# The convolution half of an encoder's output product on two scaled fp16 parts per operand, with its weight rows loaded raw

## The chip, the cores and the metric

The kernel runs on one core of a Trainium2 chip. A core has a matrix engine (TensorE, PE in the profile), a vector engine (VectorE, DVE), a scalar engine (ScalarE, ACT), a general engine (GpSimd, POOL) and a sync engine (SyncE, SP) that here only issues transfers. Each engine runs its own instructions in order; semaphores hold an instruction back until what it reads is there and what it overwrites is no longer needed. Transfers run on 16 DMA engines; in this kernel SP issues the plain ones and POOL those that change the type or add into their target, each in a queue of its own.

The metric is device time in microseconds of one execution. The time before is the median of three.

## The reference

The reference is an encoder trunk of two layers in float32 (1024 positions, width 1024). What matters here is the second half of the mixer: eight attention heads make 512 channels, a convolution module makes the other 512, and their concatenation is multiplied by w_o:

```python
u = a * jax.nn.sigmoid(gt)
u = _dwconv(u, w_dw_conv[l], b_dw_conv[l])
u = jax.nn.silu(_layernorm(u, g_conv_ln[l], b_conv_ln[l]))
y = jnp.concatenate([y_attn, u], axis=-1) @ w_o[l].astype(h.dtype)
x = x + y
h2 = _rmsnorm(x, g_ffn[l])
z = _dwconv(h2 @ w_up[l].astype(h2.dtype), w_dw_ffn[l], b_dw_ffn[l])
```

The stage that changes is `u` times the lower 512 rows of w_o, and its sum with x.

## The kernel before, in words

Activations lie with channels on the 128 partitions and the 1024 positions along the free axis, in two column halves of 512. A product in full precision is made of three products: each operand is split into a high part and the remainder (low part), and high×high, high×low and low×high are summed in PSUM. Parts are either f32r (a float32 form that PE takes, shown as `fp32r` where an engine writes it and `f32` at PE) or fp16 pairs with a power-of-two scale.

A layer has four stages. **Project** (`project`; in the profiled execution about 0 to 200 us in layer 0, 1095 to 1295 in layer 1) makes the queries, keys and the gated convolution input, section by section (q0, q1, q2, then k0, k1 ...). While it runs, VectorE applies the taps of the depthwise convolution (`conv_step`), and some taps are made on ScalarE and added into the tile by a POOL transfer (`tap_far`, tile `far`). A clock of planned PE time (`clock["pe"]`) decides when weights are asked for: `supply` issues a cast (POOL transfer, `cast`) LEAD ahead of need and turns it into a pair TURN ahead (`complete`). **Attention** (to 410 and 1505 us) makes the heads' outputs `ys`. The **output stage** (`feed`, from `wo_steps`; 410 to 496 us and 1505 to 1590 us) is a list of steps: `steps[n]()` emits PE's work of step n, and then everything that was `put` at (n, rank) is emitted in order of rank. Order of emission is each engine's order. The **up and down products** follow in the same list.

The steps of the output stage are: heads of the first column half in steps 0 to 3 (step 0 is done earlier, in attention), heads of the second half in 4 to 6, convolution blocks of the first half in 7 to 10, the last heads block in 11, convolution blocks of the second half in 12 to 15. Each block makes two of the eight 128-row output tiles: per tile 4 channel blocks times 3 parts, 12 matmuls of 512 columns (`accumulate`, L979 to L985), tile `po`. After a heads block VectorE adds x to it (`add_heads`, L1019); after a convolution block it adds it into the same tile (`evict`, L1023), which is stored, squared on ScalarE and summed for the next norm.

The weights of both halves come as f32r pairs made by POOL and ACT. `cast_pair` (L944) takes a 128×2×512 tile, and a POOL transfer writes the cast to its first half; `complete` (L201 to L204) has ScalarE write the negative of it to the second half (L202), and a second POOL transfer adds the source into that (L203). The heads' half (part 1, tag `m`, 8 slots) is cast in attention, from step WO_AT of its own agenda on, and the last ones are completed at step −1 of the list. The convolution half (part 0, tag `ws`, 8 slots) is cast at steps 0 and 1, rank 5, and completed at steps 2 and 3, rank 2. In the same steps SP loads rows of w_up (`fetch`, L1134, tile `wu`), whose squares give scales (`first_squares`).

The convolution operand comes from `conv_norm` (from L2013): `mean` and `square` at step 0, sums at 1 and 2, the root of the variance (`rstd`, tiles `lnr0t`, `lnr0v`) at step 3, its spread over the partitions (`lnr0s`) at step 4, then per column half `scale` (L2044, VectorE, then SiLU on ScalarE), `close` (L2048, ScalarE, high part `us_jh`) and `rest` (L2053 to L2055, VectorE, low part `us_jl`). Each `us` part is a float32 tile of 1024 columns under tag `b`.

Tags are slots of SBUF that are used in turn: `b` has 31 of them for most 1024-column tiles, `ws` 8, `m` 8, `wr` 3 (SLOTS, L59). The step products `scales` (L911 to L928) find the scale of the value weights and of the next norm's gain from sums of squares that `weight_squares` (L894) and the matmul with ones made; all of it at section n2 of project.

What a planner decides is only the clock in project; in the output stage the order is written by hand in steps and ranks.

Of the kernel before, what the change touches and what calls it, by code (L numbers as in the profile page):

```python
# [9 lines left out]
F32 = mybir.dt.float32  # L10
# [7 lines left out]
T = 1024  # L18
# [54 lines left out]
END_TURNS = 1  # L73
P_SCALE = 32768.0
# [64 lines left out]
class Encoder:  # L139
# [274 lines left out]
    def first_sections(self, l, supply):  # L414
# [14 lines left out]
        nc.scalar.activation(out=self.cp.tile([128, 1], F32, name="table"), in_=self.ones[:, 0:1], func=AF.Square)  # L429
# [83 lines left out]
        nc.gpsimd.tensor_copy(out=self.cp.tile([128, 1], F32, name="held"), in_=x[2][:, 0:1])  # L513
# [46 lines left out]
    def project(self, l, carry):  # L560
# [10 lines left out]
        qk = self.cp.tile([128, 8], F32, name=f"qk{l}", tag="qk", bufs=1)  # L571
        col = lambda i, n=1: qk[:, i:i + n]
# [42 lines left out]
        def launch(steps, n=-1):  # L615
            active.append([clock["pe"], steps, n])
# [229 lines left out]
        scales = {1: lambda: st.update(squares=self.weight_squares(l, w["v"])),  # L846
                  2: lambda: st.update(scale=self.scales(l, st.pop("squares")))}
# [21 lines left out]
        gain_squares()  # L869
        launch(gate(0), -3)  # L870
# [21 lines left out]
        return u, conv, away, (qd, qrd, kd, krd), (kvs, w["v"], st["scale"]), heads  # L892

    def weight_squares(self, l, w):  # L894
        nc, par = self.nc, self.par[l]
        f = self.cp.tile([128, 20], F32, name=f"sc{l}", tag="sc", bufs=1)
# [4 lines left out]
        nc.scalar.activation(out=f[:, 8:16], in_=par[:, P_GFFN:P_GFFN + 8], func=AF.Square, accum_out=f[:, 2:3])  # L901
        return f
# [8 lines left out]
    def scales(self, l, f):  # L911
        nc = self.nc
        ps = self.bank(f"sc{l}p", (128, 3))
        nc.tensor.matmul(ps, self.ones, f[:, 0:3], start=True, stop=True)
        col = lambda i: f[:, i:i + 1]
        nc.vector.tensor_copy(out=f[:, 2:5], in_=ps)
        nc.vector.tensor_tensor(out=col(3), in0=col(2), in1=col(3), op=ALU.add)
        self.half_exponent(f[:, 5:7], f[:, 3:5])
        self.power(col(0), col(5), -1.0, 200.0)
        self.power(col(1), col(5), 1.0, 39.0)  # L920
        self.power(col(7), col(6), -1.0, 197.0)
        nc.vector.tensor_scalar(out=col(16).bitcast(I32), in0=col(6).bitcast(I32), scalar1=EXPONENT, scalar2=-20.0 * EXPONENT,
                                op0=ALU.mult, op1=ALU.add)
        nc.vector.tensor_copy(out=col(17), in_=col(16).bitcast(I32))
        nc.vector.tensor_scalar(out=f[:, 8:16], in0=self.par[l][:, P_GFFN:P_GFFN + 8], scalar1=col(7), scalar2=None, op0=ALU.mult)
        nc.vector.tensor_scalar(out=col(18), in0=col(17), scalar1=-2.0 ** 31, scalar2=None, op0=ALU.add)
        self.gs, self.back, self.nback = f[:, 8:16], col(17), col(18)
        return col(0), col(1)  # L928

    def layer(self, l, carry):  # L930
        with self.psum(f"mix{l}", ([f"w{i}" for i in range(3)], 1), 2):
            mixed = self.project(l, carry)
        with self.psum(f"attn{l}", 2, 4):
            casts, ready = {}, {}
            ahead = {WO_AT: lambda: [casts.update({m: self.wo_cast(l, m, 1)}) for m in range(4)],
                     **{58 + m: lambda m=m: ready.update({(1, m): self.complete(*casts.pop(m))}) for m in range(3)},
                     61: lambda: (ready.update({(1, 3): self.complete(*casts.pop(3))}), [casts.update({m: self.wo_cast(l, m, 1)}) for m in range(4, 8)])}
            begun = {"x": {}, "po": {}}
            begun["turn"] = lambda: ready.update({(1, m): self.complete(*casts.pop(m)) for m in range(4, 4 + END_TURNS)})
            conv, ys = mixed[1], self.attention(l, *mixed, ahead, ready, begun)  # L940
        with self.psum(f"ffn{l}", 0, ([f"d{i}" for i in range(8)], 1)):
            return self.feed(l, conv, ys, ready, casts, begun["x"])()
# [10 lines left out]
    def feed(self, l, conv, ys, ready, casts, x):  # L953
# [6 lines left out]

        self.wo_steps(l, conv, ys, ready, casts, x, steps, put)
# [25 lines left out]
    def wo_steps(self, l, conv, ys, w, casts, x, steps, put):  # L987
# [33 lines left out]
        def evict(c, m):  # L1021
            xm = x[m, c]
            nc.vector.tensor_tensor(out=xm, in0=ps.pop((c, m)), in1=xm, op=ALU.add)  # L1023
# [699 lines left out]
    def attention(self, l, u, conv, away, spill, kvs, loaded, ahead, wo, begun):  # L1723
# [7 lines left out]
        def rows(tt):  # L1731
            (kv, wv, _), ts = kvs, slice(tt * 128, (tt + 1) * 128)
# [280 lines left out]
    def conv_norm(self, l, conv, out, put):  # L2013
# [34 lines left out]
        def close(j, c):  # L2048
            if c == 0:
                out.append([self.blk(f"us{l}_{j}{i}", F32R) for i in "hl"])  # L2050
            nc.scalar.copy(out=out[j][0][:, HALVES[c]], in_=st[j, "z"][:, HALVES[c]])

        def rest(j, c):  # L2053
            hi, lo = (t[:, HALVES[c]] for t in out[j])
            nc.vector.tensor_tensor(out=lo, in0=st[j, "z"][:, HALVES[c]], in1=hi.bitcast(F32), op=ALU.subtract)  # L2055
# [84 lines left out]
```

## Time and profile before

| | us |
|---|---|
| median of three runs | 2208.74 |
| lowest and highest of them | 2208.42, 2209.5 |
| the profiled execution | 2208.39 |
| its span | 2206.6 |
| mean granted clock of PE | 0.999 |

The profile is one execution. Its page gives busy times by engine, the span in 40 slices, the DMA queues, the chain of work that ended last and the costliest groups of instructions; further views give a timeline of each engine, the instructions of a line or tile, and busy time by stretch. In a group the form is `line engine operation out<-in, partitions x elements and type, count | busy us, mean ns of one | idle time before them, what ended it`. A matmul's duration overlaps its neighbours', so its rate is read from start to start. `[3.67 <-PE lnr0t L278]` behind a timeline row says that the engine stood idle for 3.67 us and that PE's work of line 278 on tile lnr0t ended this. The page's row of the w_o transfers:

```profile
wo<-in_w_o POOLq DMA_DIRECT2D x64, 256.0 KB, 7.4
```

These are 16 per half and layer: eight casts and eight adding transfers, 7.4 us from issue to landing in the median.

### The profile page before, as it was taken

Reading aid. Unit: us, or ns where it says so; the run is one execution under the profiler, and the core shown is the slowest. Engines: PE = TensorE matmul, PEld = TensorE weight load, DVE = VectorE, ACT = ScalarE, POOL = GpSimd, SP = SyncE. Lnnn points to the kernel's source line nnn. Section 1 sums busy time; section 2 is a strip of 40 time slices with the busy share of each in tenths; the row PEclk is TensorE's granted clock in tenths of the full one; section 3 lists DMA queues with packets and bytes.
Section 4 is the critical chain, followed back from the end, with each engine's and each line's share of the span. In section 5 each row is a group of like instructions: output and inputs, shape, how many; then the busy total and the mean of one; then the engine's idle time right before and its main releaser. Section 6 shows DMA issues by size and latency. Waiting matters only on the chain.

```text
span 2206.6 us, 29859 instructions
## 1 busy us (share of the span) xinstructions
PE 2196.8 (100%) x10770; PEld 1320.0 (60%) x10770; DVE 1831.5 (83%) x2506; ACT 1468.9 (67%) x2207; POOL 592.7 (27%) x546
## 2 busy tenths in 40 slices
PE   9999999999999999999999999999999999999998
PEld 8887666784444444644488876667744444446445
DVE  7989888778988887787859788887798888878877
ACT  6455987746898886554623569786468887865544
POOL 1221799511121111000012227983111111110000
PEclk9999999999999999999999999999999999999999
DMA  6896887954588886554558968789646988856533
GB/s 193 165 176 176 167 166 156 289 141 115 137 243 257 223 258 155 191 170 155 167 134 168 192 151 176 154 182 237 169 104 143 258 240 241 239 142 218 183 116 120
DMA packets 163269, 400.96 MB, mean 182 GB/s; under 512 B 22144, under 2 KB 30192, under 8 KB 163120
## 3 DMA queue, kind: packets, MB, share of 16 engines
q0 software_dynamic: 67136, 154.28, 37.8%
q1 hardware_dynamic: 95696, 244.24, 32.5%
q8 instruction: 84, 1.38, 0.3%
q10 hardware_dynamic: 288, 0.53, 0.1%
q14 instruction: 65, 0.53, 0.1%
HBM read 270.75 MB, written 69.66 MB: 154 GB/s over the span
## 4 chain that ended last, share of the span: by engine, by line
PE 97%; DVE 1%; ACT 1%; issue 0%; DMA 0%; DVEq 0%; ACTq 0%
PE p L1251 36%; PE pd L1496 17%; PE po L985 7%; PE s L1760 7%; PE o L1823 5%; PE t L1800 5%; PE pq L239 3%; PE pa L239 3%; PE pg L239 2%; PE pkv L239 2%; PE pg L557 2%; PE pn L239 1%; PE pk L239 1%; PE pa L557 1%; PE pv L1736 1%; PE pu L239 1%
## 5 line engine op out<-in xcount | busy, mean ns | idle before, releaser
L1251 PE MATMUL p<-b,w 128*128 128x512 f16 x3696 | 804.0, 379 | 0.0
L1251 PEld LDWEIGHTS <-w 128*128 128x128 f16 x3696 | 361.6, 99 | 427.4 <-issue 1.1
L1496 PE MATMUL pd<-ab,wd 128*128 128x512 f16 (+2 forms) x1920 | 404.2, 373 | 0.0
L1142 POOL DMA_DIRECT2D wu<-in_w_up x176 | 152.6, 881 | 743.2 <-DVE w L1215 540.3
L1496 PEld LDWEIGHTS <-wd 128*128 128x128 f16 x1656 | 161.9, 98 | 179.4 <-issue 0.5
L1803 DVE SCALAR_TENSOR_TENSOR pt<-t,pt 128x512 f16<-128x512 f32 x256 | 163.8, 681 | 34.8 <-ACT pt L1802 33.7
L1760 PE MATMUL s<-k,q 96*128 96x512 f16 x768 | 186.9, 379 | 0.0
L1215 DVE SCALAR_TENSOR_TENSOR w<-wu,wf,w 128x512 f16<-128x512 f32 (+1 forms) x216 | 177.2, 834 | 3.9 <-ACT w L1212 3.9
L1994 POOL TENSOR_TENSOR late<-gate,par 128x1016 f32<-128x1016 f32 (+11 forms) x79 | 170.9, 2164 | 0.0
L1802 ACT ACTIVATE pt<-t 128x512 f16<-128x512 f32 x256 | 139.1, 597 | 45.9 <-PE t L1800 45.2
L1212 ACT ACTIVATE w<-wu,wf 128x512 f16<-128x512 f32 (+1 forms) x216 | 164.8, 781 | 0.1
L1762 DVE TENSOR_REDUCE mx<-s 128x1 f32<-128x1024 f32 x128 | 155.3, 1213 | 0.0
L1485 ACT ACTIVATE ab<-ac,ds 128x512 f16<-128x512 f32 x108 | 75.5, 716 | 108.5 <-DVE ac L1400 72.9
L1770 ACT ACTIVATE p<-s,mx 128x1024 f32<-128x1024 f32 x128 | 143.4, 1121 | 1.2 <-DVE mx L1762 0.8
L1977 DVE SCALAR_TENSOR_TENSOR conv<-gate,par,conv 128x1009 f32<-128x1009 f32 (+14 forms) x110 | 139.8, 1274 | 3.5 <-ACT conv L641 0.8
L1800 PEld LDWEIGHTS t<-ident,p 128*128 128x128 f32 x1024 | 120.0, 141 | 25.7 <-ACT p L1770 1.1
L1800 PE MATMUL t<-ident,p 128*128 128x128 f32 x1024 | 133.4, 273 | 0.6 <-ACT p L1770 0.6
L1823 PE MATMUL o<-pt,v 128*128 128x512 f16 x512 | 130.8, 379 | 0.0
L1708 DVE SCALAR_TENSOR_TENSOR o<-zg,par,o 128x1023 f32<-128x1023 f32 x88 | 112.7, 1281 | 8.9 <-ACT o L1702 7.4
L1259 DVE SCALAR_TENSOR_TENSOR zg<-p,wf,zg 128x512 f32<-128x512 f32 x72 | 54.0, 750 | 72.0 <-PE p L1251 62.3
L1760 PEld LDWEIGHTS <-q 96*128 96x128 f16 x768 | 74.1, 97 | 64.5 <-issue 2.1
L1708 DVE SCALAR_TENSOR_TENSOR v<-zv,par,v 128x1023 f32<-128x1023 f32 x88 | 112.1, 1276 | 0.0
(2173 smaller groups left out, 3936.7 us busy)
## 6 DMA issues: line engine op xcount, KB each, us to landing
wu<-in_w_up SPq DMA_DIRECT2D x98, 512.0 KB
wu<-in_w_up POOLq DMA_DIRECT2D x176, 256.0 KB, 4.8
sd<-in_w_down SPq DMA_DIRECT2D x44, 512.0 KB
ws<-sd SPq DMA_DIRECT2D x44, 512.0 KB
act<-v SPq DMA_DIRECT2D x36, 512.0 KB
ac<-act SPq DMA_DIRECT2D x72, 256.0 KB
wo<-in_w_o POOLq DMA_DIRECT2D x64, 256.0 KB, 7.4
x_mix<-y SPq DMA_DIRECT2D x32, 256.0 KB
```

Of the source, the lines that this page charges most:

```text
L239: nc.tensor.matmul(ps[:, HALVES[c]], w, x[:, HALVES[c]], start=(k == 0 and s == 0), stop=(k == n - 1 and s == 2))
L1212: nc.scalar.activation(out=t, in_=src, func=AF.Copy, scale=scale[f])
L1215: nc.vector.scalar_tensor_tensor(out=t, in0=src, scalar=scale[f], in1=hi, op0=ALU.mult, op1=ALU.subtract)
L1251: nc.tensor.matmul(ps, w[p][:, k * 128:(k + 1) * 128], b[:, q], start=(i in (1, 5, 2) and k == 0 and t == 0), stop=(k == 3 and t == 2), sk ...
L1496: nc.tensor.matmul(ps[t, m][:, cs], w[i, j][p][:, m * 128:(m + 1) * 128], b[:, q, cs], start=(i in (1, 5, 2) and j == 0 and s == 0), stop= ...
L1708: self.nc.vector.scalar_tensor_tensor(out=o[:, a:b], in0=z[:, at + a:at + b], scalar=self.par[l][:, tap:tap + 1], in1=o[:, a:b], op0=ALU.m ...
L1760: nc.tensor.matmul(ps[:, cs], q[0:96, i, qs], k[0:96, j, cs], start=(s == 0), stop=(s == 2))
L1762: nc.vector.tensor_reduce(out=mx, in_=ps, op=ALU.max, axis=AX.X, negate=True)
L1800: nc.tensor.transpose(tp[:, i, qi * 128:(qi + 1) * 128], st["p"][2 * qp + qi][:, kt * 128:(kt + 1) * 128], self.ident)
L1803: nc.vector.scalar_tensor_tensor(out=lo, in0=tp, scalar=P_SCALE, in1=hi, op0=ALU.mult, op1=ALU.subtract)
L1823: nc.tensor.matmul(po, v[2 * c + i][:, h // 2, e, :], pt[s][:, 2 * (c % 2) + i, :], start=(c == 0 and i == 0 and s == 0), stop=(c == 3 and ...
L1994: self.nc.gpsimd.tensor_tensor(out=p[:, lo:hi], in0=u[:, lo + s:hi + s], in1=self.tap(l, j, t).broadcast_to([128, hi - lo]), op=ALU.mult)
```

## The change

The convolution half of the output product takes fp16 pairs on both sides, each under a power-of-two scale. The scale of the weights (`wscale`) and of the operand (`uscale`) come from sums of squares of the raw weight rows and of the layer norm's gain and bias, and the product is scaled back (`uback`) when it is evicted.

- *Squares in project.* Four loads on SP, 512 KB each, bring the rows to `b` tiles at planned clock 56, 66, 76 and 86 (`out_squares`, called at the top of each section of project); 24 later ScalarE squares each and sums it. Three small ScalarE squares of gains run at the start of project (`gain_squares`; one of them was in `weight_squares`).
- *Scales.* `scales` keeps five small VectorE operations; the rest of it and what gives the new scales moves to `more_scales` (12 small VectorE operations), at step 2, rank 4.2 of the output stage. The matmul with ones goes from 3 to 9 columns.
- *Weights of the output stage.* Instead of eight casts, eight ScalarE copies and eight adding transfers: four SP loads of 512 KB into `ws` tiles at steps 0 to 3, rank 5; four ScalarE operations (`upper`) of 128×1024 at steps 3, 3, 4, 5 and four VectorE operations (`lower`) at steps 3, 4, 5, 6 that write fp16 pairs.
- *Operand.* `close` scales on ScalarE, `rest` becomes a scalar-tensor-tensor operation, and both parts of a block lie in one `b` tile. `evict` becomes a scalar-tensor-tensor operation.
- The tile of scales grows from 20 to 32 columns, and two tiles of one column share a buffer.

```diff
+SCALES_AT = 2, 4.2
+OUT_FROM, OUT_STEP, OUT_WAIT = 56.0, 10.0, 24.0
+WO_LOAD = (0, 1, 2, 3)
+WO_UPPER = (3, 2), (3, 2.1), (4, 2), (5, 2)
+WO_LOWER = (3, 4), (4, 2), (5, 2), (6, 2)
...
+        outs = [(OUT_FROM + OUT_STEP * i, i, None) for i in range(4)]
...
+        def out_squares(now):
+            while outs and outs[0][0] <= now:
+                at, i, t = outs.pop(0)
+                if t is None:
+                    outs.append((at + OUT_WAIT, i, self.out_rows(l, i, "b")))
+                    outs.sort(key=lambda e: e[0:2])
+                else:
+                    nc.scalar.activation(out=t, in_=t, func=AF.Square, accum_out=sc[:, 3 + i:4 + i])
...
         for n, (name, weight, emit, evict, after) in enumerate(seq):
             supply(clock["pe"])
+            out_squares(clock["pe"])
...
+    def gain_squares(self, l, f):
+        par = self.par[l]
+        for i, at, n, by in ((2, P_GFFN, 8, 1.0), (7, P_GLN, 4, 32.0), (8, P_BLN, 4, 2.0)):
+            self.nc.scalar.activation(out=f[:, 21:21 + n], in_=par[:, at:at + n], func=AF.Square, scale=by, accum_out=f[:, i:i + 1])
...
+    def more_scales(self, l, f):
...
+        nc.vector.tensor_reduce(out=col(15), in_=f[:, 3:7], op=ALU.add, axis=AX.X)
+        nc.vector.tensor_tensor(out=col(16), in0=col(7), in1=col(8), op=ALU.add)
+        self.half_exponent(col(18), col(2))
+        self.half_exponent(f[:, 19:21], f[:, 15:17])
+        self.power(f[:, 27:29], f[:, 19:21], -1.0, 204.0)
+        self.power(f[:, 30:32], f[:, 19:21], 1.0, 50.0)
+        nc.vector.tensor_tensor(out=col(30), in0=col(30), in1=col(31), op=ALU.mult)
+        self.wscale, self.uscale, self.uback = (col(i) for i in (27, 28, 30))
...
+    def out_rows(self, l, i, tag):
+        t = self.tmp(tag, f"wor{l}_{i}{tag}", F32, (128, 2, 512))
+        self.nc.sync.dma_start(out=t, in_=self.a["w_o"][l, 2 * i:2 * i + 2, :, HALVES[1]].rearrange("m p c -> p m c"))
+        return t
...
+        put(*SCALES_AT, scales)
...
-        def cast(part, m):
-            casts[part, m] = self.wo_cast(l, m, part)
...
+        def load(i):
+            casts[i] = self.out_rows(l, i, "ws")
+
+        def upper(i):
+            t = self.tmp("ws", f"wo{l}_0{i}", F16, (128, 2, 2, 512))
+            nc.scalar.activation(out=t[:, :, 0], in_=casts[i], func=AF.Copy, scale=self.wscale)
+            for e in range(2):
+                w[0, 2 * i + e] = [t[:, e, p] for p in range(2)]
+            half["wo", i] = t
+
+        def lower(i):
+            t = half.pop(("wo", i))
+            nc.vector.scalar_tensor_tensor(out=t[:, :, 1], in0=casts.pop(i), scalar=self.wscale, in1=t[:, :, 0],
+                                           op0=ALU.mult, op1=ALU.subtract)
...
-        for m in range(8):
-            put(m // 4, 5, lambda m=m: cast(0, m))
-            put(2 + m // 4, 2, lambda m=m: turn(0, m))
+        for i in range(4):
+            put(WO_LOAD[i], 5, lambda i=i: load(i))
+            put(*WO_UPPER[i], lambda i=i: upper(i))
+            put(*WO_LOWER[i], lambda i=i: lower(i))
...
-            nc.vector.tensor_tensor(out=xm, in0=ps.pop((c, m)), in1=xm, op=ALU.add)
+            nc.vector.scalar_tensor_tensor(out=xm, in0=ps.pop((c, m)), scalar=self.uback, in1=xm, op0=ALU.mult, op1=ALU.add)
...
-                out.append([self.blk(f"us{l}_{j}{i}", F32R) for i in "hl"])
-            nc.scalar.copy(out=out[j][0][:, HALVES[c]], in_=st[j, "z"][:, HALVES[c]])
+                t = self.blk(f"us{l}_{j}", F16, (128, 2, T))
+                out.append([t[:, i] for i in range(2)])
+            nc.scalar.activation(out=out[j][0][:, HALVES[c]], in_=st[j, "z"][:, HALVES[c]], func=AF.Copy, scale=self.uscale)
...
-            nc.vector.tensor_tensor(out=lo, in0=st[j, "z"][:, HALVES[c]], in1=hi.bitcast(F32), op=ALU.subtract)
+            nc.vector.scalar_tensor_tensor(out=lo, in0=st[j, "z"][:, HALVES[c]], scalar=self.uscale, in1=hi,
+                                           op0=ALU.mult, op1=ALU.subtract)
```

More of the change, by code (lines that the diff above doesn't have):

```diff
@@ L428, in first_sections @@
             nc.tensor.matmul(warm, self.ones, self.ones, start=True, stop=True)
-        nc.scalar.activation(out=self.cp.tile([128, 1], F32, name="table"), in_=self.ones[:, 0:1], func=AF.Square)
+        nc.scalar.activation(out=self.cp.tile([128, 1], F32, name="table", tag="table", bufs=1), in_=self.ones[:, 0:1], func=AF.Square)
         def load(i, c):
@@ L845, in project @@
             add(f"u{i}", "u2", ranked("u2", i, QL, f"u{i}", cqs), lambda i=i: query_rope(1) if i else iter(()), held if i else norm)
-        scales = {1: lambda: st.update(squares=self.weight_squares(l, w["v"])),
-                  2: lambda: st.update(scale=self.scales(l, st.pop("squares")))}
+        scales = {1: lambda: self.weight_squares(l, w["v"], sc),
+                  2: lambda: (st.update(scale=self.scales(l, sc)))}
         for j in range(4):
@@ L869, in project @@
         gain_squares()
+        self.gain_squares(l, sc)
         launch(gate(0), -3)
@@ L891, in project, with weight_squares @@
         work(1e9)
-        return u, conv, away, (qd, qrd, kd, krd), (kvs, w["v"], st["scale"]), heads
-    def weight_squares(self, l, w):
+        return u, conv, away, (qd, qrd, kd, krd), (kvs, w["v"], st["scale"], sc), heads
+    def weight_squares(self, l, w, f):
         nc, par = self.nc, self.par[l]
-        f = self.cp.tile([128, 20], F32, name=f"sc{l}", tag="sc", bufs=1)
         for k in range(2):
@@ L912, in scales @@
         nc = self.nc
-        ps = self.bank(f"sc{l}p", (128, 3))
-        nc.tensor.matmul(ps, self.ones, f[:, 0:3], start=True, stop=True)
+        ps = self.bank(f"sc{l}p", (128, 9))
+        nc.tensor.matmul(ps, self.ones, f[:, 0:9], start=True, stop=True)
         col = lambda i: f[:, i:i + 1]
[L916 to L919, printed above, removed]
@@ L941, in layer @@
         with self.psum(f"ffn{l}", 0, ([f"d{i}" for i in range(8)], 1)):
-            return self.feed(l, conv, ys, ready, casts, begun["x"])()
+            return self.feed(l, conv, ys, ready, casts, begun["x"], begun_scales)()
     def cast_pair(self, src, name, tag):
```

32 lines of the change are left out of this document (19 added, 13 removed).

## The prediction

> **What bounds the kernel now.** I read the page first: its busy times and the chain that ended last.
>
> ```profile
> span 2206.6 us, 29859 instructions
> ...
> PE 2196.8 (100%) x10770; PEld 1320.0 (60%) x10770; DVE 1831.5 (83%) x2506; ACT 1468.9 (67%) x2207; POOL 592.7 (27%) x546
> ...
> PE 97%; DVE 1%; ACT 1%; issue 0%; DMA 0%; DVEq 0%; ACTq 0%
> ```
>
> The view of PE's waits has one in the output stage:
>
> ```profile
> PE po L985 <- DVE wt L1163: 0.5, 2, 0.3
> ```
>
> TensorE (PE) is busy for 2196.8 of 2206.6 us, and 97% of the last-ending chain is its own work. So the time falls only if PE's own work gets shorter, and all waiting of PE together is below 10 us. Any other engine or queue counts only through a stall that it gives PE. The profiled execution took 2208.39 us, 1.8 more than its span; the sum is made against 2208.39, and the median of the three runs, 2208.74, lies 0.35 above it.
>
> Next, the timeline of PE in the stage that changes, and in the next product, whose operands are already fp16. Columns: start, duration, engine, line, operation, out<-in, shape, count.
>
> ```profile
> 445.01 0.39 PE L985 MATMUL po<-us_0h,wo 128*128 128x512 f32 x1
> 445.24 0.39 PE L985 MATMUL po<-us_0l,wo 128*128 128x512 f32 x1
> ...
> 450.23 0.40 PE L985 MATMUL po<-us_3h,wo 128*128 128x512 f32 x1
> ...
> 579.70 12.47 PE L1251 MATMUL p<-b,w 128*128 128x512 f16 x57
> ```
>
> The 0.39 is a pipelined duration; what counts is the step from start to start. From 445.01 to 450.23 lie 23 steps (two accumulations of 12 matmuls, so 24 starts): 5.22/23 = 0.2267 us per f32r matmul. The fp16 row holds 57 matmuls in 12.47 us; less one duration (0.38) over 56 steps this is 0.2159 us. The view of line 985 counts the convolution half for the whole kernel:
>
> ```profile
> L985 PE MATMUL po<-us_0h,wo x64: 389/389/500, 445.0 to 1587.8; 128*128 128x512 f32 x64
> ...
> L985 PE MATMUL po<-us_0l,wo x32: 387/389/398, 445.2 to 1587.5; 128*128 128x512 f32 x32
> ```
>
> That is 96 for one of four channel blocks, so 384 in all, 192 per layer.
>
> **The change part by part.** *The matmuls.* The same 384 matmuls of 512 columns remain (two parts by two, less low times low), each 0.2267 − 0.2159 = 0.0108 us shorter: 384 × 0.0108 = **4.1 us gained**, 2.07 per layer, half of it from the columns' first half (steps 7–10), the rest from steps 12–15. This is the only edit that shortens PE. The Trainium skill, "TensorE: Matmul & The Clock Gate", section "Wait — 56ns, not 53.3ns?", gives back-to-back matmuls a gap of N ÷ 2.4 GHz + about 2.5 ns, 215.7 ns at N = 512, without a term for the operands' type; by that the old matmuls would also step at 216 ns and the gain would be 0. The fp16 row agrees with it to 0.2 ns, the f32r rows lie 11 ns above it, so the trace speaks for a cost of the type; the rule is a rival below.
>
> *What leaves other engines.* 16 POOL transfers of 256 KB per layer (eight casts, eight adding transfers) and eight ACT copies between them. None is on PE's chain, so I count 0 for their absence.
>
> *The four early loads and squares (project).* The planned times 56 to 86 don't say when SP gets there: its queue is in order.
>
> ```profile
> 77.72 6.42 SPq L656 DMA_DIRECT2D sin<-rope_tables  x8
> ...
> 152.20 0.30 SPq L147 DMA_DIRECT2D krd<-krs  x1
> ...
> 1111.58 3.97 SPq L656 DMA_DIRECT2D sin<-rope_tables  x8
> ```
>
> SP issues the sin loads until 84.1 and then nothing until 152.2. The four loads are emitted in that stretch of the program, so all 2.1 MB go out in a burst at 84 to 86 us (in layer 1 at about 1115.6). Table by stretch: sum, PE, PEld, DVE, ACT, POOL (with counts), granted clock, DMA share, GB/s.
>
> ```profile
> 88.00:92.00 4.00, 4.00 (x20) 3.30 (x19) 3.08 (x3) 2.41 (x3) 1.65 (x2) 1.00 1.06 210
> ...
> 1110.00:1120.00 10.00, 10.00 (x46) 8.29 (x45) 0.00 (x0) 0.00 (x0) 0.00 (x0) 1.00 0.43 96
> ```
>
> In layer 1 the DMA engines are half free: no cost. In layer 0 they are full. What is late there:
>
> ```profile
> L1984 POOL DMA_DIRECT2D conv<-far x2: 861/862/863, 85.7 to 86.8; - x2
> DMA to landing us min/median/max: 6.9/8.1/9.4
> ...
> L1977 DVE SCALAR_TENSOR_TENSOR conv<-gate,par,conv x1: 1267/1267/1267, 100.1 to 100.1; 128x1009 f32<-128x1009 f32 x1
> ```
>
> The last adding transfer issues at 86.8 and lands at 96.1 or 96.2; DVE's next tap on that tile starts at 100.1, a slack of 4.0. Bounds of the delay: 0 (SP's bytes pass beside POOL's) and 2.1 MB/210 GB/s = 10 us (they all go first). Halved service over its 9.4 us would be 9.4 late. I take the middle, 4.7, so DVE is 4.7 − 4.0 = 0.7 late at 100. The Trainium skill, "DMA: Bandwidth & Descriptors", section "Queues, rings and completion order", says each DMA engine takes turns between its queues packet by packet; so a new queue would take part of POOL's service at once instead of using leftovers. By it the delay would stand nearer 9.4 than 0, and the stall below nearer 5 us; no run here shows it yet.
>
> The lateness travels through krt, and one square joins it:
>
> ```profile
> 135.41 1.06 ACT L711 ACTIVATE krt<-krt 32x1024 f32<-32x1024 f32 x1 [2.69 <-DVE krt L710]
> ...
> 142.53 1.13 ACT L730 ACTIVATE cqs_0h<-cq,par 128x1024 fp32r<-128x1024 f32 x1
> ...
> 143.70 1.28 DVE L732 SCALAR_TENSOR_TENSOR cqs_0l<-cq,par,cqs_0h 128x1024 fp32r<-128x1024 f32 x1 [3.37 <-ACT cqs_0h L730]
> ...
> 156.70 1.26 DVE L732 SCALAR_TENSOR_TENSOR kvs_0l<-ckv,par,kvs_0h 128x1024 fp32r<-128x1024 f32 x1
> ...
> 159.52 0.62 PE L239 MATMUL pk<-kvs_0l,wk0h 128*128 128x512 f32 x2
> ...
> 423.02 1.04 ACT L1158 ACTIVATE wsq<-wu 128x1024 f16<-128x1024 f32 x1
> 423.97 0.19 ACT L1158 ACTIVATION_READ_ACCUMULATOR wsq<-wu 128x1 f32 x1
> ```
>
> ACT waits for DVE at 135.41, DVE for ACT at 143.70; the second square (about 1.2 us, by the same operation at 423.02) falls on ACT between the two, the others before and after. kvs_0l ends at 157.96, PE takes it at 159.52: slack 1.56. So PE stalls for 0.7 + 1.2 − 1.56 = **0.3 us**; bounds 0 (no delay) and 6 + 1.2 − 1.56 = 5.6. Layer 1 shows no full DMA, and the square alone stays under a slack of this size: 0.
>
> *The four loads of the output stage.* At steps 0–3 SP gets 2.1 MB in place of POOL's later 16 transfers, 1.57 MB of it (loads 0–2) among the w_up loads of 401 to 406, ahead of what POOL still adds for the heads' half:
>
> ```profile
> 401.42 33.88 SPq L1136 DMA_DIRECT2D wu<-in_w_up  x8
> ...
> 400.00:412.00 12.00, 11.89 (x64) 8.38 (x63) 9.56 (x16) 6.72 (x12) 3.13 (x4) 1.00 1.11 362
> 412.00:420.00 8.00, 8.00 (x37) 6.64 (x36) 7.50 (x12) 4.86 (x6) 4.75 (x9) 1.00 1.15 280
> ...
> L203 POOL DMA_DIRECT2D wo<-in_w_o x1: 892/892/892, 407.1 to 407.1; - x1
> DMA to landing us min/median/max: 8.0/8.0/8.0
> ...
> 416.02 0.39 PE L985 MATMUL po<-ys_1h,wo 128*128 128x512 f32 x1
> ...
> L203 POOL DMA_DIRECT2D wo<-in_w_o x2: 872/876/879, 1501.8 to 1504.5; - x2
> DMA to landing us min/median/max: 4.5/5.2/5.9
> ...
> 1510.47 0.39 PE L985 MATMUL po<-ys_1h,wo 128*128 128x512 f32 x1
> ```
>
> Slacks: 407.1 + 8.0 = 415.1 against 416.02, 0.9 us; in layer 1, 1501.8 + 5.9 = 1507.7 against 1510.47, 2.8 us. The engines are oversubscribed from 400 to 420 already, so SP's extra bytes mostly lengthen that stretch behind POOL's transfer rather than thin it out. Lowest 0; highest 1.57 MB ahead at 210 GB/s = 7.5 us late. I take 0.3 us in layer 0 and 0 in layer 1.
>
> *Splits, scales, evictions.* The split costs ACT 4 × 1.13 and DVE 4 × 1.28 per layer (rows of cqs_0), the 12 small scale operations about 0.17 each, 2 us; and where DVE subtracts or adds, a multiply comes with it:
>
> ```profile
> L1023 DVE TENSOR_TENSOR y<-po,y 128x512 f32<-128x512 f32 x32 | 21.2, 685 | 5.5 <-PE po L985 5.5
> ...
> L1259 DVE SCALAR_TENSOR_TENSOR zg<-p,wf,zg 128x512 f32<-128x512 f32 x72 | 54.0, 750 | 72.0 <-PE p L1251 62.3
> ...
> 427.54 1.29 DVE L289 TENSOR_REDUCE lnr0v<-lnr0t 128x4 f32<-128x512 f32 x2 [3.67 <-PE lnr0t L278]
> ...
> 433.87 2.72 DVE L2044 SCALAR_TENSOR_TENSOR conv<-conv,par,lnr0s 128x512 f32<-128x512 f32 x4 [2.43 <-PE lnr0s L316]
> ...
> 439.77 0.69 DVE L1019 TENSOR_TENSOR y<-po,y 128x512 f32<-128x512 f32 x1 [1.38 <-PE po L985]
> ...
> 443.01 0.68 DVE L2055 TENSOR_TENSOR us_0l<-lnsg,us_0h 128x512 fp32r<-128x512 f32 x1
> ```
>
> The scales fit into DVE's wait of 3.67, two lower parts into it and the 2.43, the third into the 1.38. Only the fourth, 1.2 by step, lies behind 439.77, in front of us_0l, which ends at 443.69 and is read at 445.24: slack 1.55. With 0.07 more for the multiply 0.3 stays, and I take 0.1 per layer, **0.2 us**; bounds 0 and 1.2 per layer, if one more of them slips behind 439.77. In the evictions 16 × 0.065 = 1 us per layer lies beside PE, in waits like the 5.5 of L1023.
>
> *Buffers.* The loads take four of the 31 slots for long tiles during project, and give four back in the output stage (us on one tile each): 0.
>
> **Sum:** −4.1 + 0.3 + 0.3 + 0.2 = −3.3. 2208.39 − 3.3 = 2205.1, and 0.35 for the median: **2205.4 us**; its own range, with the give-back from 0 to 1.9, is 2204.0 to 2206.5.
>
> **The rivals.** *Nothing given back, and a little more:* all 4.1 stay, and the two waits for wt, 0.5 together, go too, as the order on DVE in front of them changes: 2208.39 − 4.1 − 0.5 + 0.35 = 2204.1. For it: slack everywhere but three places. Against: those three.
>
> *The early burst:* SP's 2.1 MB go first at 84 us, POOL's additions come 10 us late, DVE 6 late, PE 5.6 before k0: 2208.39 − 4.1 + 5.6 + 0.35 = 2210.2. For it: share 1.06; against: 362 GB/s at 400, 152 above 210, so the engines can carry SP's bytes beside POOL's.
>
> *The heads' weights late (slower):* loads 0–2 go before POOL's additions at 407 and 1502. At 210 GB/s 7.5 us late: 6.6 + 4.7 lost, 2208.39 − 4.1 + 11.3 + 0.35 = 2215.9; at the stretch's own 280 GB/s 5.6 late, 4.7 + 2.8, 2212.1. It costs from 0.9 us of lateness on, and exceeds the gain from 3.9 (3.0 + 1.1). For it: shares of 1.11 and 1.15; against: loads 1 and 2 stand behind w_up loads that pass today in the same stretch, and layer 1's slack is triple.
>
> *No gain:* the type doesn't set the step (something else in that stage makes 0.227): 2208.39 + 0.8 + 0.35 = 2209.5. Against: 23 even steps.
>
> **How the numbers follow.** Forecast 0.48, nothing given back 0.10, early burst 0.17, heads late 0.20, no gain 0.05. A measurement of this kernel can tell about 0.2%, 4.4 us, from no change: below 2204.3 lie the second case and the edge of the first (0.12): faster 0.22. Above 2213.2 lies most of the heads' case (0.15), with both bursts together in it: slower 0.15. Between, 0.63. The range leaves out most of that 0.15, as it ends at the heads' lower price, and reaches 0.7 below the second case, for waits of PE not listed here: 2203.4 to 2212.2.
>
> **What would show it.** Right: the step of line 985's convolution half at 0.216, PE busy about 4 us less, k0 and the heads' matmuls within half a microsecond of their gaps now. Wrong: the four raw loads not together at 84; the additions of 86.8 landing after 101; idle PE before po<-ys_1h at 416 or before po<-us_0l; a step that stays at 0.227.

## The result, and the profile after

| | before | after |
|---|---|---|
| median, us (15 runs each) | 2208.66 | 2204.32 |
| lowest and highest | 2208.42, 2209.5 | 2203.98, 2206.31 |
| profiled execution, its span | 2208.39, 2206.6 | 2204.32, 2202.5 |

The ratio after to before is 0.998, with a 95% interval from 0.9973 to 0.9988: 4.3 us, or 0.2%, faster. The forecast was 2205.4 with a range from 2203.4 to 2212.2, and for the likeliest case alone 2204.0 to 2206.5.

The page of the changed kernel, its span and busy times:

```profile
span 2202.5 us, 29874 instructions
...
PE 2193.2 (100%) x10770; PEld 1286.3 (58%) x10770; DVE 1844.9 (84%) x2528; ACT 1478.9 (67%) x2223; POOL 568.8 (26%) x514
```

PE runs as many instructions as before and is busy 3.6 us less; VectorE and ScalarE have 13 and 10 us more, POOL 24 us and 32 instructions less. The waits of PE that the profile names:

```profile
PE warm L433 <- DVE ones_r L409: 1.1, 1, 1.1
PE t L1852 <- ACT p L1822: 0.6, 2, 0.3
PE kt L601 <- ACT rkv L693: 0.6, 2, 0.3
PE po L1024 <- DVE wt L1215: 0.5, 2, 0.3
PE rx_768p L274 <- ACT xsq_e L1560: 0.2, 1, 0.2
```

The columns are total, times, longest. None is at k0, at the heads or at us, where the forecast had put 0.8 us. What is new is small and elsewhere: the wait at xsq_e in the last norm, and 0.1 more at kt than before:

```profile
PE kt L585 <- ACT rkv L677: 0.5, 2, 0.2
```

The stage itself, PE's timeline at its two ends in both layers, first before, then after (the first row of each layer is the first convolution matmul, the last row the first of the up product):

```profile
445.01 0.39 PE L985 MATMUL po<-us_0h,wo 128*128 128x512 f32 x1
...
495.59 0.60 PE L1251 MATMUL p<-b,w 128*128 128x512 f16 x2
...
1539.47 0.39 PE L985 MATMUL po<-us_0h,wo 128*128 128x512 f32 x1
...
1590.02 0.39 PE L1251 MATMUL p<-b,w 128*128 128x512 f16 x1
```

```profile
445.44 4.92 PE L1024 MATMUL po<-us,wo 128*128 128x512 f16 x22
...
493.78 1.03 PE L1303 MATMUL p<-b,w 128*128 128x512 f16 x4
...
1537.92 0.61 PE L1024 MATMUL po<-us,wo 128*128 128x512 f16 x2
...
1586.27 0.59 PE L1303 MATMUL p<-b,w 128*128 128x512 f16 x2
```

Layer 0 took 495.59 − 445.01 = 50.58 us and takes 493.78 − 445.44 = 48.34; layer 1 took 50.55 and takes 48.35. That is 2.24 + 2.20 = 4.44 us gained in the stage. Outside it PE gives back some of this: it starts the stage 0.43 later in layer 0 (0.30 of this arise in the program's first 6 us, ahead of every new load) and needs 0.26 more between the two stages (1044.14 against 1043.88). PE's last matmuls of the program, before and after, show the rest:

```profile
2198.00 1.94 PE L1613 MATMUL end<-ident,x 128*128 128x128 f32 x16
```

```profile
2194.68 1.95 PE L1665 MATMUL end<-ident,x 128*128 128x128 f32 x16
```

They start 3.32 us earlier. So of the 4.44 gained, 1.1 are given back up to there: the 0.43, the 0.26, and another 0.43 between layer 1's stage and these matmuls. From their start to the end of the span it takes 8.6 us before and 7.8 after, and these 0.8 make up the difference of the spans, 4.10. Nothing of the change touches that stretch. It takes 7.8 to 8.1 us in the traces of all ten kernels below too, so the one trace of before stands apart there; why is open.

The step: 22 matmuls in 4.92 us, less one duration (0.38) over 21 steps, is 0.2162 us against 0.2267. Over 384 that gives 4.0; the other 0.4 must lie in the passages between kinds of matmuls; they were not traced further.

### The profile page after: what moved, and what is told of

It is laid out like the page before. It is cut to its first block, busy times and chain, and to the rows that moved or that the text cites. A ratio compares the mean times of both kernels' runs of the same rounds, so it can differ in the third digit from the quotient of the medians.

```text
span 2202.5 us, 29874 instructions
## 1 busy us (share of the span) xinstructions
PE 2193.2 (100%) x10770; PEld 1286.3 (58%) x10770; DVE 1844.9 (84%) x2528; ACT 1478.9 (67%) x2223; POOL 568.8 (26%) x514
## 4 chain that ended last, share of the span: by engine, by line
PE 97%; DVE 1%; ACT 1%; issue 0%; DMA 0%; DVEq 0%; ACTq 0%
PE p L1303 36%; PE pd L1548 17%; PE s L1812 7%; PE po L1024 7%; PE o L1875 5%; PE t L1852 5%; PE pq L244 3%; PE pa L244 3%; PE pkv L244 2%; PE pg L244 2%; PE pg L562 2%; PE pn L244 1%; PE pk L244 1%; PE pa L562 1%; PE pv L1788 1%; PE pu L244 1%
```

## The experiments

All were timed in turn with the kernel before, on one chip each time; times below are medians, to be held against 2204.32 for the changed kernel. Differences of a few tenths of a microsecond between kernels of different groups are near what these medians can tell.

### Is it the type alone? f32r parts on the change's path

```diff
-            t = self.tmp("ws", f"wo{l}_0{i}", F16, (128, 2, 2, 512))
-            nc.scalar.activation(out=t[:, :, 0], in_=casts[i], func=AF.Copy, scale=self.wscale)
+            t = self.tmp("ws", f"wo{l}_0{i}", F32R, (128, 2, 512))
+            nc.scalar.activation(out=t, in_=casts[i], func=AF.Copy, scale=self.wscale)
...
-                t = self.blk(f"us{l}_{j}", F16, (128, 2, T))
-                out.append([t[:, i] for i in range(2)])
+                out.append([self.blk(f"us{l}_{j}{i}", F32R) for i in "hl"])
```

> The changed kernel with every load, square, scale, split and eviction in its new place; only the parts of the convolution half are f32r again (one of the four raw loads and the operand parts use slots of the long tiles, as f32r parts need twice the room). Theory (the whole gain is the shorter step of 384 fp16 matmuls): step back at 0.2267 us, time 4.1 to 4.4 us above the changed kernel's 2204.3, so 2208.4 to 2208.8. Rival (part of the gain comes from POOL's 32 transfers that are gone, or from the loads asked for early): the time stays below 2207.5.

Measured: 2208.73 (ratio to before 1.0, 0.9991 to 1.0009). PE's timeline of this kernel, the first and the last of two accumulations:

```profile
446.07 0.39 PE L1027 MATMUL po<-us_0h,wo 128*128 128x512 f32 x1
...
451.28 0.40 PE L1027 MATMUL po<-us_3h,wo_00l 128*128 128x512 f32 x1
```

23 steps in 5.21 us, 0.2265 each. With all transfers, squares and splits in their new places, and 32 POOL transfers fewer, the whole gain is gone with the type. So the gain is the step of the matmul, and by the medians the new path as a whole takes as long as the old one. PE itself reaches its last matmuls 1.6 us later than before in this kernel (2199.62 against 2198.00), and behind them it needs 7.9 us instead of 8.6.

### What the early loads and squares cost

One kernel without the loads and the squares, one with the loads and without the squares; both set the sums by a constant.

```diff
-        outs = [(OUT_FROM + OUT_STEP * i, i, None) for i in range(4)]
+        outs = []
+        nc.vector.memset(sc[:, 3:7], 0.25)
```

> The changed kernel without the four early loads of 512 KB per layer and without their squares; the sums of squares are set by a constant, so the weights' scale is not computed. Theory (the burst only eats slack): 2204.1, between 0 and 0.3 us below the changed kernel; the adding transfer of far issued near 87 us lands after about 9.4 us instead of 12.2, and kvs_0l is ready 1.5 us before PE reads it instead of 0.6. Rival (the burst costs PE time): 2203.7 or lower.

```diff
+        nc.vector.memset(sc[:, 3:7], 0.25)
...
-                    nc.scalar.activation(out=t, in_=t, func=AF.Square, accum_out=sc[:, 3 + i:4 + i])
+                    pass
```

> The changed kernel with the four early loads per layer but without their squares; the sums of squares are set by a constant. It parts the 0.57 us between the changed kernel (2204.32) and the one without loads and squares (2203.75). Theory (the squares on ScalarE are what PE's wait for rkv at kt and for xsq_e in the last norm grew by): 2203.8. Rival (the burst's contention is): 2204.3.

Measured: 2203.75 without both, 2203.90 with the loads alone. The changed kernel, with both, is some 0.6 us slower, where 0 to 0.3 were expected. But by the traces only a part of this is due to them. PE's last matmuls start 0.70 later in the changed kernel than in the one without both, and of this 0.22 arise in the first 31 us, ahead of every early load, and 0.36 in the last norm, behind a pause of VectorE that is looked at below and that three later kernels with the squares don't have. What comes with the squares is some 0.2 us at kt, over both layers: PE's wait there is 0.6 in the kernels that have them, and without them it is back at the value of before. The row of the kernel with the loads alone:

```profile
PE kt L602 <- ACT rkv L694: 0.5, 2, 0.2
```

The burst itself does what it was feared for, in this trace without reaching PE. The view of the adding transfers of far, issued at 85.8 to 87.1, in the kernel without early loads and in the changed one:

```profile
L2037 POOL DMA_DIRECT2D conv<-far x2: 857/860/862, 85.8 to 86.8; - x2
...
DMA to landing us min/median/max: 7.1/8.2/9.3
```

```profile
L2036 POOL DMA_DIRECT2D conv<-far x2: 857/860/862, 86.1 to 87.1; - x2
...
DMA to landing us min/median/max: 10.0/11.1/12.2
```

The later one lands after 12.2 us instead of 9.3, at 87.1 + 12.2 = 99.3; VectorE's run of taps is unbroken there. Of the slack of 4.0, 2.9 are used. This is one execution: in the traces of all kernels with this one burst the later transfer lands after 12.2 (twice), 13.0 (twice), 13.1, 13.3, 13.5, 13.9 and 14.3 us, so the delay by one burst runs from 2.9 to 5.0 us, and the forecast 4.7 lies within.

### The burst doubled

```diff
+                    if i == 3:
+                        for _, j, t in [e for e in outs if e[2] is not None]:
+                            nc.sync.dma_start(out=t, in_=self.a["w_o"][l, 2 * j:2 * j + 2, :, HALVES[1]].rearrange("m p c -> p m c"))
```

> The changed kernel with each of the four early loads issued twice into the same tile, so 4.2 MB instead of 2.1 MB on SP from 85 us on. Theory (each DMA engine shares its service between the queues; 2.8 us of the slack of 4.0 is eaten by the first burst): the far transfer issued near 87 lands 0 to 3 us later than in the changed kernel, the tap at 100.4 starts 0 to 1.8 us late, the slack of 0.6 before k0 is used up, and the time is 0 to 1.2 us above 2204.3. Rival (SP's bytes go ahead of POOL's): 2.1 MB more at 210 GB/s, 10 us later, some 8 us above: 2212.

Measured: 2208.07 (2206.53 to 2209.78), 3.75 above the changed kernel. Neither forecast holds. The transfer lands 1.9 us later than in the changed kernel's trace, and the tap is late by the expected size; but 14.1 us lie within what one burst alone gives, 12.2 to 14.3, so what the second burst adds to the landing is not shown. The rows of the far transfers, of VectorE and of PE's waits in this kernel:

```profile
DMA to landing us min/median/max: 12.0/13.1/14.1
```

```profile
100.95 6.50 DVE L2032 SCALAR_TENSOR_TENSOR conv<-gate,par,conv 128x1009 f32<-128x1009 f32 x5 [0.73 <-DMA conv<-far]
...
130.24 1.22 DVE L721 TENSOR_TENSOR krt<-pkr,krt 64x1024 f32<-64x1024 f32 x1 [2.70 <-ACT krt L719]
```

```profile
PE kt L604 <- ACT rkv L696: 2.1, 2, 1.8
PE pk L244 <- DVE kvs_0l L751: 1.4, 1, 1.4
```

The 0.73 would have cost little. What costs is a second path, on ScalarE:

```profile
123.95 1.06 ACT L207 ACTIVATE wq20l<-wq20h 128x1024 fp32r<-128x1024 f32 x1 [2.75 <-DMA wq20h<-in_w_in]
```

ScalarE waits for a weight that comes late by POOL's queue (its cast is issued at 113.4 us, and at 108.1 to 110.3 in the kernels with one burst), and behind this wait, in its order, stand the first square, three far copies and the krt copy; VectorE then waits 2.70 us for krt at 130.24, and PE 1.8 (0.3 in the changed kernel) and 1.4 us. So k0's danger was real and its end was where the prediction put it, but its way ran through the weights' casts and ScalarE's order, and not through the tap that the prediction watched.

### The output stage's loads first

```diff
-WO_LOAD = (0, 1, 2, 3)
+WO_LOAD = (-2, -2, -2, -2)
```

> The changed kernel with all four loads of the output stage at step -2, ahead of the w_up rows, instead of at steps 0 to 3. Theory (sharing between the queues; the heads' last weights have 0.8 us of slack in layer 0 and 0.5 in layer 1): the adding transfers issued near 407 and 410 land 0.5 to 2 us later, PE stalls for 0 to 1.5 us per layer, 2204.3 to 2207. Rival (SP's bytes ahead of POOL's): 2.1 MB at 362 GB/s are 5.8 us, less the slack 5.0 and 5.3 us: about 2214.6.

Measured: 2204.30, no difference. The landing of the addition issued at 407.5 in the changed kernel, and of the one issued at 407.4 in this one:

```profile
DMA to landing us min/median/max: 8.1/8.1/8.1
```

```profile
DMA to landing us min/median/max: 7.5/7.5/7.5
```

It does not land later when 2.1 MB stand before the w_up rows instead of among them. In the changed kernel the weights are there at 407.5 + 8.1 = 415.6, and PE reads them at 416.43: 0.8 of slack, as in the forecast.

Layer 1 is where the loads cost the heads' weights something. The changed kernel's additions there, and PE's first reading of the second:

```profile
L208 POOL DMA_DIRECT2D wo<-in_w_o x2: 872/876/879, 1500.0 to 1503.0; - x2
...
DMA to landing us min/median/max: 7.1/7.6/8.1
```

```profile
1511.62 0.39 PE L1024 MATMUL po<-ys_1h,wo 128*128 128x512 f32 x1
```

The second lands 8.1 us after 1503.0, at 1511.1, with 0.6 of slack. Before the change it took 4.5 us from 1504.5, with PE reading at 1513.19: 4.1 of slack. In the kernel with all loads in front it takes 8.4 us, and at most 0.3 of slack is left. So the rival's delay does happen in layer 1, by some 3.6 us, and the slack just swallows it.

### The slack in front of us

The changed kernel's VectorE between the heads and us:

```profile
440.20 0.69 DVE L1071 TENSOR_TENSOR y<-po,y 128x512 f32<-128x512 f32 x1 [0.21 <-PE po L1024]
440.81 1.27 DVE L1053 SCALAR_TENSOR_TENSOR wo<-wor_3ws,sc,wo 128x1024 f16<-128x1024 f32 x1
442.00 2.71 DVE L2096 SCALAR_TENSOR_TENSOR conv<-conv,par,lnr0s 128x512 f32<-128x512 f32 x4
444.64 2.73 DVE L2108 SCALAR_TENSOR_TENSOR us<-lnsg,sc,us 128x512 f16<-128x512 f32 x4
```

The four low parts of us take 0.68 each from 444.64 on, so the first is there at 445.3; PE reads it with its second matmul, at 445.44 + 0.22 = 445.66. That is some 0.3 us. The test moves one more of the lower parts in front:

```diff
-WO_LOWER = (3, 4), (4, 2), (5, 2), (6, 2)
+WO_LOWER = (3, 4), (4, 2), (6, 2), (6, 2)
```

> The changed kernel with the third lower part (VectorE, 1.28 us) moved from step 5 to step 6, so that two instead of one lie in front of us. Theory (the low parts of us have 0.2 to 0.3 us of slack in front of PE, and VectorE's chain there is what sets it): PE stalls for 1.2 less 0.25, about 0.95 us per layer, time 2206.2 (2205.8 to 2206.5). Rival (the slack read from the rows is not the real one, since PE or ScalarE sets the chain): 2204.3 as before.

Measured: 2206.39, 2.07 above, as the theory has it. Its waits:

```profile
PE po L1024 <- DVE us L2108: 1.6, 2, 0.8
```

0.8 us in each layer, and a slower first step behind each. One part in the wrong place costs half of the change's gain.

### What the xsq_e wait is

In the changed kernel VectorE stands still once at the end, between two sums of squares, with no one to wait for but itself:

```profile
2176.84 0.69 DVE L264 TENSOR_TENSOR xss<-xss,xsq 128x512 f32<-128x512 f32 x1 [0.46 <-DVE xss L264]
```

```diff
+        nc.vector.memset(sc[:, 29:30], 0.0)
```

> The changed kernel with one more tiny VectorE instruction per layer, a memset of an unused column at the start of project; all else the same. It tests what 0.3 of the 0.42 us between the changed kernel and the one without squares are: in the changed kernel VectorE stands 0.456 us between two sums of squares at 2176.84 with nothing that it waits for, the last norm is that much later, and PE waits for xsq_e; in the two runs with a memset per layer the gap is gone from there. Theory (the gap belongs to a place in VectorE's stream of instructions, not to the squares): 2204.0, PE's wait for xsq_e gone, the wait for rkv at kt still 0.6 in two. Rival (the squares cause it): 2204.3, both waits there.

Measured: 2204.14; both waits are still there, and so is the gap, but it has moved one sum ahead:

```profile
2175.78 1.49 DVE L264 TENSOR_TENSOR xss<-xss,xsq 128x512 f32<-128x512 f32 x2 [0.46 <-DVE xss L262]
```

The added instructions shift the gap, as a place in VectorE's stream would have it; that they would take it off the sums, and the wait with it, failed. The records of the traces say more: counted from VectorE's first record, its waits included, the operation behind the gap is number 3264 in all six kernels that show the gap, and 3264 stands one sum earlier where two records were added. In the six that show none, before among them, record 3264 directly follows an operation, or is itself a wait. It is the place and not the squares: the three kernels below have the squares and no gap. Why that place is slow, by some 0.35 us more than the usual 0.1 between these sums, stays open.

### The same edit on the heads' half

Since 384 matmuls of the heads' half still step at 0.227, the next kernel gives them fp16 parts too. The heads' outputs stay at the scale of the values (a constant takes the place of the values' scale back), `add_heads` becomes a scalar-tensor-tensor operation, and all scales are found in project again.

```diff
-            ahead = {WO_AT: lambda: [casts.update({m: self.wo_cast(l, m, 1)}) for m in range(4)],
...
+            ahead = {55: lambda: (load(0), load(1)), 58: lambda: upper(0), 59: lambda: (lower(0), upper(1)), 60: lambda: lower(1),
+                     61: lambda: (load(2), load(3))}
...
+            begun["turn"] = lambda: upper(2)
...
+        put(-1, 3, lambda: head_upper(3))
+        put(-1, 3.5, lambda: head_lower(2))
+        put(1, 3, lambda: head_lower(3))
```

> The changed kernel with the same edit on the heads' half too: its weight rows loaded raw by SP, split by ScalarE and VectorE into scaled fp16 pairs in attention and steps -1 to 1, the heads' outputs left at the scale of the values and split to fp16, x added with a scale; all scales found in project. The weights' scale is the one found from the convolution half's rows. Theory (a type's step is worth 10.8 ns per matmul wherever the split is hidden): 384 more matmuls, 4.1 us below 2204.3, so 2200.2, up to 2202 where 2 us of the splits are not hidden. Rival (VectorE and ScalarE are too full at the end of attention; four lower parts of 1.28 us per layer and their waits reach PE): 2204 to 2214.

Measured: 2208.89, as slow as before: the rival's side. What it costs is in three views of this kernel: PE's waits, VectorE's timeline, and the windows behind the wait (sum, PE, PEld, DVE, ACT, POOL, granted clock, DMA share, GB/s).

```profile
PE rc_0s L321 <- DVE rc L1929: 4.4, 2, 2.2
```

```profile
395.13 3.02 DVE L982 SCALAR_TENSOR_TENSOR wo<-wor_1h,sc,wo 128x1024 f16<-128x1024 f32 x1
398.07 0.17 DVE L1929 RECIPROCAL rc<-sums 128x4 f32<-128x4 f32 x1
```

```profile
399.50:401.00 1.50, 1.50 (x5) 0.53 (x4) 1.50 (x2) 0.42 (x1) 0.00 (x0) 0.54 1.06 384
401.00:402.50 1.50, 1.50 (x7) 1.25 (x6) 0.20 (x2) 1.37 (x3) 0.00 (x0) 0.50 1.05 386
402.50:404.00 1.50, 1.50 (x10) 1.01 (x9) 1.37 (x3) 1.19 (x2) 0.00 (x0) 0.82 1.04 385
```

The second lower part stands in front of the reciprocal, and it takes 3.02 us instead of 1.28. POOL works at the same time, on a split of the heads' outputs with two operands in SBUF:

```profile
394.95 2.12 POOL L1909 TENSOR_TENSOR ys_5l<-yt,ys_5h 128x1024 f16<-128x1024 f32 x1 [5.67 <-ACT ys_5h L1908]
```

That ends at 397.07, 1.94 us after VectorE's operation began, and 3.02 is 1.94 plus 1.08. The Trainium skill, "SBUF — State Buffer", section "SBUF: two separate sides", states that a VectorE operation with two SBUF inputs and a GpSimd operation that reads SBUF share a pair of ports: whichever starts first holds it for its whole instruction and blocks the other. The rows fit it, and so does layer 1, where VectorE took 3.01 us and ended 1.08 us behind POOL. Behind the wait of 2.2 us PE's granted clock is 0.54, 0.50 and 0.82 for 4.5 us, which by these shares (0.46 + 0.50 + 0.18, times 1.5 us) costs 1.7 us more; in layer 1, after as long a wait, it stayed at 1.00.

So the places were wrong, not the number of operations. The next kernel moves them:

```diff
-            ahead = {55: lambda: (load(0), load(1)), 58: lambda: upper(0), 59: lambda: (lower(0), upper(1)), 60: lambda: lower(1),
+            ahead = {52: lambda: (load(0), load(1)), 56: lambda: upper(0), 57: lambda: lower(0), 59: lambda: upper(1),
...
-            begun["turn"] = lambda: upper(2)
+            begun["turn"] = lambda: (upper(2), lower(1))
```

> The kernel with the heads' half on fp16 too, its loads and split moved: the first pair's loads and parts three steps earlier, the second pair's lower part after the end of the scores instead of in front of the reciprocal rc that PE waited 2.2 us for in each layer. Theory (the loss there was VectorE's order, plus some 2 us at a lower granted clock behind the wait in layer 0, 0.77 and 0.66 in the two stretches of 3 us behind it): 4.4 + 1.9 less than 2208.9, 2202.6, between 2201.5 and 2204. Rival (VectorE is too full there for any place): 2206 or more.

Measured: 2201.44 (ratio to before 0.9967, 0.9955 to 0.9979), just below the 2201.5 to 2204 expected. The wait for rc is gone, and the largest that stand in the heads' and the output stage now are these:

```profile
PE o L1890 <- DVE pt L1870: 0.8, 2, 0.5
PE po L1040 <- DVE us L2129: 0.8, 2, 0.4
```

The second is the slack in front of us again: PE gets there a microsecond earlier, and VectorE does not. But the last of the four pairs of weights is read only some 15 us after the first, so its lower part need not stand there.

This trace also shows what the prediction feared for k0, with the one burst of the changed kernel. The landings of far, issued at 85.8 and 86.8, VectorE's tap, and PE's reading of kvs_0l:

```profile
DMA to landing us min/median/max: 12.0/13.1/14.3
```

```profile
101.11 6.50 DVE L2050 SCALAR_TENSOR_TENSOR conv<-gate,par,conv 128x1009 f32<-128x1009 f32 x5 [0.86 <-DMA conv<-far]
```

```profile
160.05 0.73 PE L244 MATMUL pk<-kvs_0l,wk0h 128*128 128x512 f32 x2 [0.24 <-DVE kvs_0l L748]
```

The transfer lands at 86.8 + 14.3 = 101.1, the tap waits 0.86 us for it, and PE waits 0.24 at k0. The forecast had 0.7 and 0.3.

The next kernel moves the last lower part behind us:

```diff
-WO_LOWER = (3, 4), (4, 2), (5, 2), (6, 2)
+WO_LOWER = (3, 4), (4, 2), (5, 2), (7, 2)
```

> The kernel with both halves on fp16 (2201.44), with the last lower part of the convolution half's weights moved from step 6, in front of us, to step 7 behind it: PE first reads that pair 15 us after the first us. Theory (with PE a microsecond earlier, VectorE's chain in front of us has lost its slack, and PE's two waits for us, 0.5 each with the step, are what one part of 1.28 us there costs): both waits go, 2200.4 (2200.1 to 2200.9), and PE's two waits for wt stay at 0.5 together. Rival (VectorE is late again at wt, where 2.39 us of idle time take the part up): 2201.4 or above.

Measured: 2200.26 (ratio to before 0.9962, 0.9949 to 0.9976; 2198.9 to 2200.99 in five runs). PE has no wait for us any more, and the part fits in VectorE's idle time behind:

```profile
445.71 1.28 DVE L1066 SCALAR_TENSOR_TENSOR wo<-wor_3ws,sc,wo 128x1024 f16<-128x1024 f32 x1
448.46 0.17 DVE L1230 TENSOR_REDUCE wt<-wt 128x4 f32<-128x8 f32 x1 [1.47 <-PE wt L1241]
```

This version is 4.1 us faster than the changed kernel and 8.5 faster than before. It takes the scale of the heads' weights from the other half's rows; a kernel for any weights would have to find that too, and its loads would need another place than the burst at 85 us, as the doubled burst shows.

## Why the prediction was right

*The bound and the gain.* That another engine counts only through a stall that it gives PE held in every run. The gain was put at 384 × 0.0108 = 4.1 us; the stage gained 4.4, and the kernel with f32r parts lost all of it. The Trainium skill's gap for back-to-back matmuls ("TensorE: Matmul & The Clock Gate", section "Wait — 56ns, not 53.3ns?") describes the fp16 step, 216 ns, and not the f32r step, 227; the rival built on it is out.

*The give-back.* At PE's last matmuls 1.1 us of the 4.4 are given back, where 0.8 of 4.1 were forecast, so PE gets there 3.3 us earlier, just as forecast. That the sizes agree is partly luck: in the trace of the changed kernel the three places that were named cost nothing, and the 1.1 stand elsewhere.

- k0, 0.3 taken. In this trace far was delayed by 2.9 us, not 4.7, so the tap's slack of 4.0 held. kvs_0l is done at 159.33 and read at 159.94:

```profile
158.07 1.26 DVE L748 SCALAR_TENSOR_TENSOR kvs_0l<-ckv,par,kvs_0h 128x1024 fp32r<-128x1024 f32 x1
...
159.94 0.62 PE L244 MATMUL pk<-kvs_0l,wk0h 128*128 128x512 f32 x2
```

  Of the slack of 1.56, 0.6 is left; with the loads but without the squares it is 1.4, so the squares take most of it. In the kernel with the heads' half respaced, the same burst delayed the transfer by 5.0 us, and the forecast chain ran to its end, 0.24 us at PE. So the term has the right mechanism and size, and whether it is paid differs from one trace to the next. The Trainium skill ("DMA: Bandwidth & Descriptors", section "Queues, rings and completion order") states that each DMA engine takes turns between its queues; the landings agree, 9.3 us without the burst and 12.2 to 14.3 with it, but the delay is about half of what halved service would make, 9.4.
- The heads' weights, 0.3 taken for layer 0 and nothing for layer 1: in layer 0 the slack is 0.9 before and 0.8 after; in layer 1, where the prediction read 2.8 on the first addition, the second goes from 4.1 to 0.6. No wait, and none with all loads in front.
- us, 0.2 taken: the forecast slack of 0.3 is what is there, and a move of 1.28 us cost 0.8 of waiting per layer, as such a slack demands.

What did cost was not in the list: 0.3 us in the program's first microseconds, about 0.1 at kt with the squares, and 0.37 in the last norm, where the pause of VectorE stands. And the 0.8 us that came back behind PE's last matmuls were in no term: the median fell by 4.3 where 3.3 were forecast, and this stretch, which the change doesn't touch, is most of the difference. In the kernel with f32r parts it hides part of what PE gives back.

The forecast's own range has a slip: with nothing given back its sum is 2208.39 − 4.1 + 0.35 = 2204.6, not 2204.0, and the measured 2204.32 lies 0.3 below that.

*The rivals.* The early burst is a mechanism of this kernel; with one burst it reached PE for 0.24 us in one trace, and doubled it costs 3.75 us, by a way through POOL's casts and ScalarE's order that the prediction did not name. For the heads' weights no run produced a wait, though the delay is there in layer 1. The second rival's number, 2204.1 with nothing given back and the waits for wt gone, is the nearest to 2204.32, but by chance: those waits stand in the profile of after unchanged, 0.5 us, and PE gave back 1.1.

## What to carry to other kernels

Where PE sets the time, read the step from start to start for each type of operand, and count the matmuls: here fp16 parts instead of f32r parts save 10.5 to 10.8 ns on each matmul of 512 columns. The splits and transfers of such a rewrite show little in the time if they fit beside PE; here about 1 us was given back. They fit when each is placed by what reads it next: one operation of 1.28 us in front of PE's operand instead of behind it cost 1.0 us per layer in one test, and taking one away from there brought 0.6 in another. When a queue is loaded further, follow not only the first reader of its latest transfer, but every engine that waits for one in its own order. And a delay that is sized from one trace can be off by two microseconds: the same burst gave landings from 12.2 to 14.3 us. Last, split the gain at PE's last work before crediting it: here 0.8 of the 4.1 us between the two spans came behind it.

## What the runs showed of the hardware that was not expected

- A VectorE operation of 128×1024 with two inputs in SBUF took 3.02 us instead of 1.28 while POOL ran one of 2.12 us: it ended 1.08 us after POOL's.
- A wait of PE of 2.2 us was followed by 4.5 us at a granted clock of 0.50 to 0.82 in one layer, and by none below 1.00 in the other.
- VectorE stood still for 0.46 us between two of its own instructions, at the same record of its stream, number 3264, in six kernels, waiting for nothing that the profile shows; a further instruction per layer ahead of it moved the pause one sum earlier.
- With the same 2.1 MB on SP's queue, POOL's adding transfer landed after 12.2 to 14.3 us in nine traces, and after 9.3 to 9.4 without them.
